# DeepNorm layer with a product-key expert FFN on one core: two index lists, the pace of the row gathers, one engine's order and three late factors

## The chip, the cores and the metric

The kernel runs on one core of one Trainium2 chip. The metric is the device time of one execution in microseconds (us): the median of three timed runs before the change is 1704.05 us (1701.3 to 1706.63). The layer is float32 throughout, 256 tokens of width 2048. A change of less than 0.3%, some 5 us, can't be told from none.

## The reference, cut to what matters

The layer has three parts, each closed by a layer norm: a mixed attention (8 differential and 8 stick-breaking heads), an expert FFN found by product keys, and a gated per-layer embedding. The change lies in the FFN:

```python
def peer_ffn(x, wq, sub_keys, u, v):          # x: 256 tokens of 2048; u, v: 16384 experts of 2048
    q = (xt @ wq).reshape(t, 8, 256)           # 8 heads; halves qa, qb
    va, ia = top_k(qa . sub_keys[0], 16)       # 16 of 128 keys for each half
    vb, ib = top_k(qb . sub_keys[1], 16)
    cand = va[:, None] + vb[None, :]           # 256 pairs
    top, sel = top_k(cand, 16)
    eidx = ia * 128 + ib  at  sel              # 16 experts per token and head
    gates = softmax(top)
    w = gates * gelu(u[eidx] . x)              # 128 experts per token in all
    return sum over those 128 of  w * v[eidx]
```

## The kernel before, in words

**Stages.** The kernel goes once through these stages, and TensorE (PE) has work in each: the attention with its projections and the first norm (0 to 414 us in the profile), the 16 query projections q0 to q15 with the top-k on VectorE (DVE) beside them (414 to 533 us), 68 dense *u blocks* (533 to 864 us), 40 *row blocks* (869 to 1145 us), 86 *v blocks* (1147 to 1590 us, the last three of them in another order, see below), and the closing norm, gate and embedding.

**Two ways to the experts.** Of the 256 tokens the first 88 are *sparse*: for each, the rows u[e] and v[e] of its own experts are fetched from HBM by GpSimd (POOL) with indirect DMAs, the *gathers*, 128 rows of 8 KB (1.05 MB) at a time into one of four `gb` buffers (`NGB`). There are 88 gathers of u rows and then 88 of v rows. DVE consumes each with one instruction over 128x2048 (`use()`): a dot product with x for u (L951), and a weighted sum into `y` for v (L961, the first of a group L959). The other 168 tokens (`NDT`) are *dense*: PE multiplies them with whole blocks of 128 experts. One block is 16 fp32 matmuls of 128x128 by 128x168, which the profile counts as 32.

**u blocks and row blocks.** For the expert blocks 0 to 67 (`SEG1`) u is loaded transposed by SyncE's queue (SP) into the five `wf` buffers, multiplied, and GELU goes to A0 and A1 (`u_block`, L212). Of the other 60 blocks only the experts that some dense token uses are taken: a list of their indices is made on the core, POOL fetches those rows (`uf`, 40 row blocks of 128, `CAPS[1]`), PE transposes them (`ps_T`, L1286), ScalarE (ACT) copies the result to `uT` (L1289), PE multiplies (L1295), and GELU goes to WL.

**Gate factors.** `gate_work` builds for each dense token the matrix of its gate values over (expert block, expert): one-hot rows on DVE (`eq`, `ohb`), scaled on ACT into two fp16 halves `hi` and `lo` (L1048, L1049), a product on PE (`ps_G`), and a DVE multiply into A0 and A1. The result is written to HBM (`s_w0`, 5.9 MB; for the second part `s_w1`, 5.2 MB). This is the *first factor pass* (part 0, beside the row blocks) and the second one (part 1, beside the first v blocks).

**Lists.** `list_work(oh, part)` turns the count of users per expert (`m16`) into a compact list: column sums and ranks on PE and DVE, then 23 groups (part 0) or 20 groups (part 1) of one-hot tiles on DVE (`eqb`, `blk`, `row`) and products on PE (`ps_list`), at last the indices `idxV` (rows of u and v) and `idxW` (rows of `s_w`). Before the change part 1 is made in the u blocks, by the generator `work`, and part 0 in the row blocks, by `listing`.

**v blocks.** For each of 46 + 40 listed blocks (`CAPS`) POOL fetches the factors `wc` (128 rows of 672 B from `s_w`) and the rows `vf` (128 rows of 8 KB from v); a `vf` takes one of the five `wf` buffers, so it is fetched at most four blocks ahead (`LEAD`). For part 1 DVE multiplies wc by WL (`weigh`, L1371), and PE adds 16 products into the six banks `psv` (L1348). The last three blocks (`STAG`) are kept back as `held`: their products are issued bank by bank, so that bank after bank can be closed (`v_out`, L1363), transposed (`res2`, L1421) and taken into the statistics. Ahead of bank 2 stand the *row sums* of the sparse tokens, `third_sums`, which need the finished `y` (L1015).

**What sets the order.** The program is written stage by stage, and generators are advanced inside the block loops: `run(work, n)` does n steps of the side work, and `gathers(p)` adds p to an account and issues one gather (a step of `sparse`) for each whole unit. The paces are the constants `GQ` (q blocks from the fourth), `GU`, `GUF` (u blocks with one step and with more), `GUL`, `GULS` (row blocks up to 27, and later), `GV` (v blocks). Each engine runs its instructions in the order of its own queue. A scheduler chooses that order, except that instructions wrapped in `keep(...)` stay in written order against each other on their engine. Each gather of the u stage is preceded by a tiny `mark` load on SP and a copy on POOL, which tie POOL's place to SP's. SP's queue is in order too: a load that must wait for its buffer holds back all loads behind it. The v stage's loop ends with

```python
        if b == N1 - STAG - 1:            # the last v block ahead of the held ones
            while not run(sparse, 1):     # the rest of the sparse work
                pass
...
    held = [weigh(block)[2:] for block in fetched]
```

Of the kernel before, what the change touches and what calls it, by code (L numbers as in the profile page):

```python
# [13 lines left out]
AF = mybir.ActivationFunctionType  # L14
# [25 lines left out]
SEG1 = 68  # L40
# [4 lines left out]
CAPS = (46, 40)  # L45
# [8 lines left out]
NDT = T - NSP  # L54
# [1 line left out]
NGB = 4  # L56


GQ = 2.1
GU, GUF, GUL, GULS = 0.50, 0.60, 1.40, 1.00  # L60
GV = 0.68
GSCALE = 2.0 ** 15
GB = 3

# [96 lines left out]
def build(tc, a, out):  # L161
# [624 lines left out]
    def topk_work():  # L786
        nc.vector.tensor_copy(io128, io128f)
        for h in range(PH):
            for _ in topk_heads(0, h, 1):
                pass  # L790
            head_slots(h)
            yield
        for i in range(1, len(GROUPS)):
            slots(i, 0, by_slot(i, 0))

        second, first, flags = topk_heads(1, 0, PH), gates(0), first_flags()
        for step in range(24):
            next(second)
            if step > 2:
                next(first, None)  # L800
            next(flags, None)
            yield
        for _ in second:
            next(flags, None)
            yield
        for _ in flags:
            yield
        yield from index_T(1)
        yield from second_flags(gates(1))
# [48 lines left out]
    def second_flags(gating):  # L858

        nonlocal steps  # L860
        pools.close("tk")
        flp = pools.open("flp", "left", bufs=1)
        for dst, src in ((ahead, a["c_svalid"][:, :P]), (ones16, a["c_ones"])):
            src_f = flp.tile([P, P], F32, name="src_f", tag="src_f", bufs=2)
            load(src_f, src)
            nc.gpsimd.tensor_copy(dst, src_f)
        load(lin, a["c_lin"])
        steps = 5
        made = []

        def counts():
            t0, n, ohb, eq = made.pop(0)
            for j in range(n):
                count(t0 + j, ohb[:, j, :], eq[:, j, :])

        for i, t0 in enumerate(range(P, T, GB)):
            n = min(GB, T - t0)
            ohb = flp.tile([P, GB, P], F16, name="ohb", tag="ohb", bufs=OHB)
            eq = flp.tile([P, GB, P], F16, name="eq", tag="eq", bufs=OHB)
            if i % 2:  # L880
                for j in range(n):
                    act_one_hot(eq[:, j, :], flp, niaT[:, t0 + j:t0 + j + 1])
            else:
                keep(nc.vector.tensor_tensor(
                    eq[:, :n], io128[:, None, :].to_broadcast([P, n, P]),
                    iaT[:, t0:t0 + n, None].to_broadcast([P, n, P]), op=ALU.is_equal))
            keep(nc.vector.tensor_tensor(
                ohb[:, :n], io128[:, None, :].to_broadcast([P, n, P]),
                ibT[:, t0:t0 + n, None].to_broadcast([P, n, P]), op=ALU.is_equal))
            made.append((t0, n, ohb, eq))  # L890
            next(gating, None)
            yield
            if len(made) > OHB - 1:
                counts()
        while made:
            counts()
        keep(nc.vector.tensor_scalar(m16, cnt.pop(), 1.0, None, op0=ALU.min))
        for _ in gating:
            pass
        gates_T()  # L900
        steps = 3
        yield
        yield from list_work(flp, 1)

    ys = [None for _ in GROUPS]
    pace = gin.tile([1, 1], F32, name="pace")
# [118 lines left out]
    def gate_work(oh, parts, s0, ns, part, fresh):  # L1025
# [5 lines left out]
        def one_hot(t0, n):  # L1031
            def rows(x, m):
                return x[:, None, :].to_broadcast([P, n, m])

            def cols(x, m):
                return x[:, t0:t0 + n, None].to_broadcast([P, n, m])

            ohb = oh.tile([P, GB, P], F16, name="ohb", tag="ohb", bufs=OHB)
            eq = oh.tile([P, GB, ns], F16, name="eq", tag="eq", bufs=OHB)
            hi = oh.tile([P, GB, ns], F16, name="hi", tag="hi", bufs=OHB)  # L1040
            lo = oh.tile([P, GB, ns], F16, name="lo", tag="lo", bufs=OHB)
            keep(nc.vector.tensor_tensor(eq[:, :n], rows(io128[:, s0:s0 + ns], ns), cols(iaT, ns),  # L1042
                                         op=ALU.is_equal))
            keep(nc.vector.tensor_tensor(ohb[:, :n], rows(io128, P), cols(ibT, P),
                                         op=ALU.is_equal))
            for j in range(n):
                t = slice(t0 + j, t0 + j + 1)
                nc.scalar.mul(hi[:, j, :], eq[:, j, :], ghf[:, t])  # L1048
                nc.scalar.mul(lo[:, j, :], eq[:, j, :], glf[:, t])  # L1049
            return ohb, hi, lo  # L1050

        def product(t0, n, ohb, hi, lo):
# [185 lines left out]
    for ia in range(SEG1):  # L1238
        if ia == EARLY:
            pools.close("earlyp")  # L1240
            a1p = pools.open("a1p", "right", bufs=1)
            A1 = a1p.tile([P, SEG1 - SEG0, NDT], F32, name="A1")
        u_block(ia, W_of(ia))
        run(work, steps)
        gathers(1.5 if ia < EARLY else GU if steps == 1 else GUF)
    while not run(work, 1):
        pass
    pools.close("flp", "tkl")
# [33 lines left out]
    def rows_T(uf, c, pool, tpool):  # L1282

        ps = pbank(pool, "ps_T")
        for j in range(4):
            nc.tensor.transpose(ps[:, j * P:(j + 1) * P],  # L1286
                                uf[:, (4 * c + j) * P:(4 * c + j + 1) * P], ident)
        uT = tpool.tile([P, 512], F32, name="uT", tag="uT", bufs=4 if tpool is utp else 2)
        nc.scalar.copy(uT, ps)  # L1289
        return uT  # L1290

    def rows_mm(ps, uT, c):
# [2 lines left out]
            nc.tensor.matmul(ps[:, :NDT], uT[:, j * P:(j + 1) * P], XF[:, d, NSP:],  # L1295
                             start=d == 0, stop=d == ND - 1)

    def first_part():
        yield from gate_work(ohp, (A0, A1), *PARTS[0], 0, False)

    def first_list():
        yield from list_work(ohp, 0)

    work, listing = first_part(), first_list()
    rows = []
    turned = []

# [12 lines left out]
    for b in range(CAPS[1]):  # L1320
        if b == CAPS[1] - 5:
            while not run(work, 1):
                pass
            while not run(listing, 1):
                pass
            pools.close("a1p", "a0p")
            g2p = pools.open("g2p", "right", bufs=1)
            G2 = g2p.tile([P, SEG2, NDT], F32, name="G2")
            wcp = pools.open("wcp", "right", bufs=1)
        ps = pbank(pp, "ps_u")  # L1330
        for c in range(4):
            turn(4 * b + c + 2)
            rows_mm(ps, turned.pop(0), c)
            if b < CAPS[1] - 5:
                run(work, 1)
        nc.scalar.activation(WL[:, b, :], ps[:, :NDT], AF.Gelu_apprx_tanh)
        if b > 2:
            run(listing, 1)
        if b >= CAPS[1] - 4:
            fetch(wcp)  # L1340
        gathers(GUL if b < 28 else GULS)
# [120 lines left out]
    for b in range(LEAD + 1, N1 - STAG):  # L1462
# [8 lines left out]
        if b == N1 - STAG - 2:  # L1471

            tc.mark_branch_hint_location("rest", "LikelyTaken", [mybir.EngineType.PE])
        if b == N1 - STAG - 1:
            while not run(sparse, 1):
                pass

# [391 lines left out]
```

## Time and profile before

| | |
|---|---|
| median of three runs | 1704.05 us |
| time of the profiled execution, its span | 1705.25 us, 1703.4 us |
| PE busy | 1667.9 us (98%) |
| DVE busy, ACT busy, POOL busy | 1120.4, 754.0, 678.5 us |
| DMA | 533.47 MB, mean 313 GB/s |
| share of the DMA engines' time in POOL's queue | 48.3% |
| granted clock of PE | 0.991 |

The 1.9 us between span and time lie before the first and after the last instruction. PE is busy for 98% of the span, so time can be won or lost almost only where PE stands still or runs at a lower clock, and the profile is to be read by stage: which waits of PE there are, and which queue was late. A busy PE is not always PE at full speed; the column PEclk of the windows tells the granted clock. A DMA share of about 1 means that the 16 DMA engines moved data without a pause.

### The profile page before, as it was taken

What the parts mean: (1) busy time and instruction counts of PE and PEld (TensorE: products, weight loads), DVE (VectorE), ACT (ScalarE), POOL (GpSimd) and SP (SyncE); (2) the same over time, 40 slices, a digit from 0 to 9 for tenths busy, and PEclk for the clock granted to TensorE, in tenths of its full rate; (3) what the DMA queues carried; (4) which work ended last, traced back from release to release, by engine and by line L of the source; (5) the groups of instructions that cost most, each with busy time, mean ns of one, the idle gap of its engine ahead of it and who ended that gap; (6) DMA issues with size and microseconds to landing.
All of it is one profiled execution on the core that took longest, in us unless ns stands there. A gap on an engine that the chain in (4) does not pass through costs nothing.

```text
span 1703.4 us, 29145 instructions
## 1 busy us (share of the span) xinstructions
PE 1667.9 (98%) x11120; PEld 1549.9 (91%) x11120; DVE 1120.4 (66%) x2127; ACT 754.0 (44%) x1883; POOL 678.5 (40%) x605
## 2 busy tenths in 40 slices
PE   9999999999999999999999999999999999997998
PEld 7888888877889999999999999899999999997786
DVE  5565488763499789756768888646774343453776
ACT  5677468753101534366457776435551001000552
POOL 0144023103254423611355434555665778782000
PEclk9999999999999999999999999999999999998999
DMA  8645644484998999897799887999999999996561
GB/s 295 197 153 162 235 160 154 158 317 150 377 393 333 373 420 414 347 383 291 293 396 403 314 340 310 370 423 407 359 379 397 417 415 415 416 406 267 177 262 50
DMA packets 93976, 533.47 MB, mean 313 GB/s; under 512 B 12920, under 2 KB 16168, under 8 KB 41064
## 3 DMA queue, kind: packets, MB, share of 16 engines
q0 software_dynamic: 48912, 327.40, 48.3%
q1 hardware_dynamic: 43192, 201.02, 32.2%
q10 hardware_dynamic: 1728, 3.15, 0.5%
q8 instruction: 89, 1.46, 0.3%
q14 instruction: 55, 0.45, 0.1%
HBM read 515.70 MB, written 15.99 MB: 312 GB/s over the span
## 4 chain that ended last, share of the span: by engine, by line
PE 67%; DMA 13%; DVE 10%; issue 5%; POOL 4%; ACT 1%; POOLq 0%; SPq 0%; ACTq 0%; DVEq 0%
PE ps_v L1348 16%; PE ps_u L1295 9%; PE ps_qk L200 7%; PE ps_u L212 6%; DVE gb L951 4%; PE ps_qk L202 4%; PE ps_T L1286 4%; DMA uf<-u_rows,idxV 3%; PE ps_q L212 3%; DMA gb<-u_rows,eig 3%; DMA vf<-v_rows,idxV 3%; DMA gb<-v_rows,eig 2%; PE ps_v L219 2%; PE ps_v L220 2%; PE ps_v L221 2%
## 5 line engine op out<-in xcount | busy, mean ns | idle before, releaser
L1348 PE MATMUL ps_v<-wc,vf 128*128 128x168 f32 x2752 | 414.3, 310 | 13.5 <-DVE wc L1371 10.5
L1348 PEld LDWEIGHTS ps_v<-wc,vf 128*128 128x128 f32 x2752 | 399.0, 192 | 15.7 <-DVE wc L1371 10.8
L212 PE MATMUL ps_u<-XF,wf 128*128 128x168 f32 x2016 | 303.9, 308 | 1.2 <-DMA wf<-peer_u 1.2
L212 PEld LDWEIGHTS ps_u<-XF,wf 128*128 128x128 f32 x2016 | 288.8, 190 | 2.8 <-DMA wf<-peer_u 1.3
L122 DVE TENSOR_TENSOR wl<-wf,wh 128x1024 fp32r<-128x1024 f32 (+1 forms) x199 | 212.7, 1091 | 104.1 <-ACT wh L121 102.3
L121 ACT CAST wh<-wf 128x1024 fp32r<-128x1024 f32 (+1 forms) x199 | 172.1, 893 | 228.4 <-DMA wf<-ple_gate 114.5
L961 DVE SCALAR_TENSOR_TENSOR y<-gb,ew,y 128x2048 f32<-128x2048 f32 x78 | 182.9, 2345 | 85.9 <-DMA gb<-v_rows,eig 85.6
L951 DVE SCALAR_TENSOR_TENSOR gb<-gb,xq 128x2048 f32<-128x2048 f32 x88 | 203.0, 2318 | 45.9 <-DMA gb<-u_rows,eig 45.7
L1295 PE MATMUL ps_u<-XF,uT 128*128 128x168 f32 x1280 | 213.0, 310 | 0.0
L983 POOL DMA_INDIRECT gb<-u_rows,eig x88 | 113.8, 1294 | 217.2 <-DVE gb L951 111.7
L1295 PEld LDWEIGHTS ps_u<-XF,uT 128*128 128x128 f32 x1280 | 186.3, 191 | 0.4
L200 PE MATMUL ps_qk<-X,wh 128*128 128x512 f32 x512 | 185.2, 401 | 0.0
L983 POOL DMA_INDIRECT gb<-v_rows,eig x88 | 129.6, 1473 | 110.2 <-DVE y L961 44.6
L202 PE MATMUL ps_qk<-X,wl 128*128 128x256 f32 x512 | 145.7, 285 | 0.0
L1048 ACT ACTIVATE hi<-eq,ghf 128x68 f16<-128x68 f16 (+1 forms) x336 | 113.2, 337 | 70.3 <-DVE eq L1042 70.2
L1262 POOL DMA_INDIRECT vf<-v_rows,idxV x86 | 107.0, 1244 | 63.1 <-PE ps_G L1057 30.5
L1289 ACT COPY uT<-ps_T 128x512 f32<-128x512 f32 x160 | 91.3, 580 | 79.5 <-PE ps_T L1286 74.3
L200 PEld LDWEIGHTS ps_qk<-X,wh 128*128 128x128 f32 x512 | 96.4, 188 | 22.0 <-issue 1.0
L1262 POOL DMA_INDIRECT wc<-s_w,idxW x86 | 105.7, 1229 | 26.6 <-issue 24.4
L212 PE MATMUL ps_q<-XF,wf 128*128 128x256 f32 x512 | 113.8, 379 | 0.7 <-ACT eb L581 0.7
L1049 ACT ACTIVATE lo<-eq,glf 128x68 f16<-128x68 f16 (+1 forms) x336 | 112.1, 334 | 0.0
L212 PEld LDWEIGHTS ps_q<-XF,wf 128*128 128x128 f32 x512 | 95.8, 190 | 13.4 <-ACT eb L581 1.1
(335 smaller groups left out, 2601.1 us busy)
## 6 DMA issues: line engine op xcount, KB each, us to landing
wf<-peer_u SPq DMA_DIRECT2D x63, 1024.0 KB
wf<-w_qk SPq DMA_DIRECT2D x64, 512.0 KB
wf<-w_out SPq DMA_DIRECT2D x32, 512.0 KB
wf<-peer_wq SPq DMA_DIRECT2D x16, 1024.0 KB
wf<-ple_gate SPq DMA_DIRECT2D x16, 1024.0 KB
wf<-w_v SPq DMA_DIRECT2D x16, 512.0 KB
wf<-w_sv SPq DMA_DIRECT2D x15, 512.0 KB
early<-peer_u SPq DMA_DIRECT2D x5, 1024.0 KB
```

Of the source, the lines that this page charges most:

```text
L121: self.order(nc.scalar.copy(wh, src))
L122: self.order(nc.vector.tensor_tensor(wl, src, wh.bitcast(F32), op=ALU.subtract))
L200: nc.tensor.matmul(ps, wh[:, j * P:(j + 1) * P], xt[:, dt, :], start=dt == 0, stop=False)
L202: nc.tensor.matmul(ps[:, :T], wl[:, j * P:(j + 1) * P], xt[:, dt, :T], start=False, stop=dt == ND - 1)
L212: nc.tensor.matmul(ps[:, :T - t0], wf[:, dt * P:(dt + 1) * P], xt[:, dt, t0:], start=dt == 0, stop=dt == ND - 1)
L951: keep(nc.vector.scalar_tensor_tensor(g, g, 1.0, xq[i], op0=ALU.mult, op1=ALU.mult, accum_out=eact[i][:, j:j + 1]))
L961: keep(nc.vector.scalar_tensor_tensor(ys[i], g, ew[i][:, j:j + 1], ys[i], op0=ALU.mult, op1=ALU.add))
L983: keep(nc.gpsimd.indirect_dma_start(out=g, out_offset=None, in_=a[kind], in_offset=bass.IndirectOffsetOnAxis(ap=eig[i][:, 0, j:j + 1], axi ...
L1048: nc.scalar.mul(hi[:, j, :], eq[:, j, :], ghf[:, t])
L1262: keep(nc.gpsimd.indirect_dma_start(out=dst, out_offset=None, in_=src, in_offset=bass.IndirectOffsetOnAxis(ap=idx[:, b:b + 1], axis=0)))
L1295: nc.tensor.matmul(ps[:, :NDT], uT[:, j * P:(j + 1) * P], XF[:, d, NSP:], start=d == 0, stop=d == ND - 1)
L1348: return nc.tensor.matmul(psv[d // 3][:, d % 3 * NDT:(d % 3 + 1) * NDT], vf[:, d * P:(d + 1) * P], wc, start=False, stop=last and (d % 3 = ...
```

## The change

It has six edits.

1. *Paces.* The q blocks issue 1.6 instead of 2.1 gathers each, the u blocks 1, then 0.60, then 0.75, and 0.40 in the last eight (before: 1.5, 0.50, 0.60), the row blocks 1.45 up to block 27 and 0.60 after (before: 1.40 and 1.00), the v blocks 0.74 instead of 0.68. The number of gathers is the same, 176.
2. *Top-k work.* While it runs, every second u block does two steps of it instead of one, and there are nine steps, which only hand out flag work, between the end of the top-k of the second 128 tokens and the transposes of its indices.
3. *Lists.* `list_work(flp, 0)` follows `list_work(flp, 1)` in the u blocks at three steps a block; `listing` is gone.
4. *First factor pass.* It is advanced from row block 2 on.
5. *ACT.* `hi`, `lo`, the copy to `uT` and the GELU to WL are kept in written order.
6. *Last v factors.* The blocks that are fetched and not yet multiplied are weighed ahead of the rest of the sparse work.

```diff
-GQ = 2.1
-GU, GUF, GUL, GULS = 0.50, 0.60, 1.40, 1.00
-GV = 0.68
+GQ = 1.6
+GU, GUF, GUT, GUL, GULS = 0.60, 0.75, 0.40, 1.45, 0.60
+GV = 0.74
@@ topk_work
         for _ in second:
             next(flags, None)
             yield
+        for _ in range(9):
+            next(flags, None)
+            yield
@@ second_flags
         yield from list_work(flp, 1)
+        steps = 3
+        yield from list_work(flp, 0)
@@ gate_work, one_hot
-                nc.scalar.mul(hi[:, j, :], eq[:, j, :], ghf[:, t])
-                nc.scalar.mul(lo[:, j, :], eq[:, j, :], glf[:, t])
+                keep(nc.scalar.mul(hi[:, j, :], eq[:, j, :], ghf[:, t]))
+                keep(nc.scalar.mul(lo[:, j, :], eq[:, j, :], glf[:, t]))
@@ u blocks
-        run(work, steps)
-        gathers(1.5 if ia < EARLY else GU if steps == 1 else GUF)
+        run(work, steps + (steps == 1) * (ia % 2))
+        gathers(1 if ia < EARLY else GU if steps == 1 else GUF if ia < SEG1 - 8 else GUT)
@@ rows_T
-        nc.scalar.copy(uT, ps)
+        keep(nc.scalar.copy(uT, ps))
@@ row blocks
-            while not run(listing, 1):
-                pass
...
-            if b < CAPS[1] - 5:
+            if 2 <= b < CAPS[1] - 5:
                 run(work, 1)
-        nc.scalar.activation(WL[:, b, :], ps[:, :NDT], AF.Gelu_apprx_tanh)
-        if b > 2:
-            run(listing, 1)
+        keep(nc.scalar.activation(WL[:, b, :], ps[:, :NDT], AF.Gelu_apprx_tanh))
@@ end of the v blocks
         if b == N1 - STAG - 1:
+            fetched[:] = [weigh(block) for block in fetched]
             while not run(sparse, 1):
                 pass
```

Where instructions stand in the built programs, at three places. First DVE at the end of the v blocks, before the change. L961 is the use of a v gather, L1371 the weighing, L122 the low half of the gate weights, L1363 the closing of a bank; L1480 is a branch, and the row L1491 behind it belongs to a path that isn't taken.

```order
L1371 TENSOR_TENSOR wc<-wc,WL 128x168 x2
L961 SCALAR_TENSOR_TENSOR gb<-gb,ew_4056 128x2048 x2
L1480 COMPARE_AND_BRANCH
L1491 TENSOR_TENSOR wc<-wc,wl 128x168 x20
L1480 UNCONDITIONAL_BRANCH x2
L961 SCALAR_TENSOR_TENSOR gb<-gb,ew_4056 128x2048
L1371 TENSOR_TENSOR wc<-wc,WL 128x168 x2
L122 TENSOR_TENSOR wl<-wf,wh 128x512 x4
L1363 SCALAR_TENSOR_TENSOR XF<-XF,ps_v 128x3x168 x2
```

The same place after it (the lines are numbered anew: L966, L1366, L1358).

```order
L1366 TENSOR_TENSOR wc<-wc,WL 128x168 x2
L966 SCALAR_TENSOR_TENSOR gb<-gb,ew_4056 128x2048 x2
L1476 COMPARE_AND_BRANCH
L1487 TENSOR_TENSOR wc<-wc,wl 128x168 x20
L1476 UNCONDITIONAL_BRANCH x2
L966 SCALAR_TENSOR_TENSOR gb<-gb,ew_4056 128x2048
L122 TENSOR_TENSOR wl<-wf,wh 128x512 x4
L1358 SCALAR_TENSOR_TENSOR XF<-XF,ps_v 128x3x168 x2
```

The two weighings that stood behind the last use of a gather are now ahead of the last three uses; the closing of the banks stands behind the last use as before.

Second, POOL at the same place, before the change: L1262 fetches factors and rows of a v block, L983 is a gather.

```order
L983 DMA gb<-v_rows,eig_4054 128x2048
L1262 DMA wc<-s_w_61,idxW_7698 128x168
L1262 DMA vf<-v_rows,idxV_7697 128x2048
L983 DMA gb<-v_rows,eig_4054 128x2048
L1480 COMPARE_AND_BRANCH
```

And after it (L1267, L988).

```order
L988 DMA gb<-v_rows,eig_4054 128x2048
L1267 DMA wc<-s_w_61,idxW_7397 128x168
L1267 DMA vf<-v_rows,idxV_7396 128x2048
L988 DMA gb<-v_rows,eig_4054 128x2048 x2
L1476 COMPARE_AND_BRANCH
```

Behind the last fetch of a v block there are now two gathers instead of one.

Third, SP's queue in the u blocks, before the change. The loads at L281 bring constants for the lists (`src_f`, `lin`); the first takes the place of a table that the top-k on DVE reads to its end. The u load ahead of them is that of block 36.

```order
L111 DMA wf<-peer_u 128x2048 x2
L980 DMA mark<-c_iota 1x1
L111 DMA wf<-peer_u 128x2048
L281 DMA src_f<-c_svalid 128x128
L281 DMA src_f<-c_ones 128x128
L281 DMA lin<-c_lin 128x68
L111 DMA wf<-peer_u 128x2048
```

After it, the u load ahead of `src_f` is that of block 26.

```order
L111 DMA wf<-peer_u 128x2048
L985 DMA mark<-c_iota 1x1
L281 DMA src_f<-c_svalid 128x128
L111 DMA wf<-peer_u 128x2048
L281 DMA src_f<-c_ones 128x128
L281 DMA lin<-c_lin 128x68
L111 DMA wf<-peer_u 128x2048
```

The constants have moved ten u blocks ahead, and with them the place at which SP's loads stand behind the end of the top-k.

More of the change, by code (lines that the diff above doesn't have):

```diff
@@ L1296, in rows_mm @@
                              start=d == 0, stop=d == ND - 1)
[L1298 to L1304, printed above, removed]
+    work = gate_work(ohp, (A0, A1), *PARTS[0], 0, False)
     rows = []
```

## The prediction

> **What bounds the kernel now.** I read the page's first lines, then PE's waits, the windows, and the timelines at the places where PE waits.
>
> ```profile
> span 1703.4 us, 29145 instructions
> PE 1667.9 (98%) x11120; PEld 1549.9 (91%) x11120; DVE 1120.4 (66%) x2127; ACT 754.0 (44%) x1883; POOL 678.5 (40%) x605
> ...
> PE ps_v L1348 <- DVE wc L1371: 10.5, 1, 10.5
> PE ps_T L1286 <- DMA uf<-u_rows,idxV: 6.5, 4, 3.2
> PE ps_v L1348 <- DMA vf<-v_rows,idxV: 2.7, 3, 1.2
> ...
> PE ps_u L212 <- DMA wf<-peer_u: 1.2, 1, 1.2
> ```
>
> The waits' columns are total us, times, longest. PE is busy for 98% and its work stays the same, so only waits can be won: 10.5 us ahead of the held blocks, 6.5 for fetched u rows, 2.7 for fetched v rows, 1.2 for a u load. The windows (us; busy time of PE, PEld, DVE, ACT, POOL; granted clock; DMA share; GB/s) show where the DMA is the partner:
>
> ```profile
> 1093.00:1104.00 11.00, 7.79 (x52) 7.56 (x51) 2.35 (x1) 3.24 (x6) 4.70 (x5) 0.89 1.02 424
> 1104.00:1120.00 16.00, 15.26 (x111) 14.94 (x111) 4.70 (x2) 5.52 (x11) 2.82 (x3) 0.97 1.02 427
> ...
> 1180.00:1290.00 110.00, 110.00 (x958) 108.17 (x957) 77.89 (x144) 63.08 (x258) 71.27 (x59) 1.00 0.97 371
> ...
> 1400.00:1500.00 100.00, 100.00 (x703) 99.42 (x702) 47.36 (x50) 4.43 (x8) 79.58 (x59) 1.00 1.02 415
> 1500.00:1520.00 20.00, 20.00 (x142) 20.00 (x141) 8.67 (x12) 0.00 (x0) 16.34 (x13) 1.00 1.00 398
> 1520.00:1540.00 20.00, 20.00 (x143) 20.00 (x142) 8.45 (x8) 0.00 (x0) 15.47 (x13) 1.00 1.01 411
> ```
>
> Late in the v blocks PE and DMA are both full: 703 matmuls in 100 us are 142 ns each, 4.55 us for a block of 32, at 415 GB/s. Earlier (1180 to 1290) factor products lengthen the blocks, and the DMA moves only 371.
>
> **Start of the row blocks.**
>
> ```profile
> POOL gb L983 <- DVE eqb L1166: 20.4, 4, 12.3
> ...
> 858.13 1.19 POOL L1277 DMA_INDIRECT uf<-u_rows,idxV  x1 [0.30 <-issue]
> ...
> PE ps_T L1286 <- DMA uf<-u_rows,idxV: 2.2, 1, 2.2
> ```
>
> POOL's gathers lag behind the list on DVE, the first `uf` goes out at 858.1, and PE waits 2.2 us for it (the last row is the window 855 to 875). After the change both lists end some seven blocks ahead of the row blocks, and the last u blocks pace 0.40 gathers, so POOL is free when the buffer is, about two u blocks earlier: -2.2. If it is still late, 0. Part 0's list costs PE the same in either stage; I cost its move at nothing, because PE shows no wait for the list that is made there already. Without DVE's room there, PE's list products would hold back u blocks.
>
> **End of the row blocks.**
>
> ```profile
> 1079.77 8.89 SPq L281 DMA_DIRECT2D s_w<-A  x9
> ...
> PE ps_T L1286 <- DMA uf<-u_rows,idxV: 4.3, 3, 3.2
> ...
> L1175 DVE TENSOR_TENSOR row<-io,rank 128x384 f16<-128x384 f16 (+1 forms) x23 | 12.7, 554 | 16.7 <-PE ps_G L1057 16.7
> ```
>
> SP's factor write starts at 1079.8; then the DMA is full (424, 427), PE waits 4.3 us for `uf` (window 1080 to 1130), and at clocks 0.89 and 0.97 it loses 7.79 x 0.11 + 15.26 x 0.03 = 1.3 us more: 5.6. Before, each block brings a `uf` and a gather, 2.1 MB, beside the 5.9 MB written, plus gathers that DVE's list work made late (its `row` tiles alone take 12.7 us). After, a block brings 1.05 x 1.60 = 1.7 MB and nothing is late. Five blocks of 6.3 us at 415 GB/s move 13 MB; they need 16.4 before and 14.3 after, and `uf` runs four blocks ahead. I take -5.6, between that and 0. The later first pass moves the write by two blocks, still ahead of its first reader. ACT in written order: copies to `uT` already stand between `hi` and `lo`, and PE has no wait for ACT there, so nothing.
>
> **Middle of the u blocks.** SP stands until DVE is through the top-k:
>
> ```profile
> SPq L281 <- DVE ibN L731: 15.3, 1, 15.3
> ...
> 635.86 4.89 SPq L111 DMA_DIRECT2D wf<-peer_u  x2
> ...
> 697.75 0.33 SPq L281 DMA_DIRECT2D src_f<-c_svalid  x1
> ...
> 699.13 0.38 SPq L111 DMA_DIRECT2D wf<-peer_u  x1
> ...
> 706.67 5.54 PE L212 MATMUL ps_u<-XF,wf 128*128 128x168 f32 x37 [1.16 <-DMA wf<-peer_u]
> ...
> 539.60:697.30 157.70, 157.70 (x1124) 157.16 (x1124) 135.07 (x331) 64.25 (x189) 63.68 (x81) 1.00 0.94 377
> ...
> 539.60:697.30 157.70, 68.55 (x58) 1.00 0.94 377
> ```
>
> The last row is L951 alone on DVE (two records a gather, 29 gathers). Of 157.7 us DVE is busy for 135.1, 66.5 of them with other work than gathers, and idle for 22.6. After the change 17 uses stand in the same stretch of its queue: 66.5 + 17 x 2.36 = 106.7, plus 3 to 22.6 idle. I take 8, since 12 gathers fewer compete: the top-k ends at 654. SP meets `src_f` behind the load of block 26 (635.86), stands until 654, and block 27's load goes out at 655 and lands 7.5 us later (699.13 to 706.67), at 663. PE wants block 27 five blocks of 4.6 us after 635.9, at 659, and 1.5 later for flag counts that now come earlier. It waits 2.3 instead of 1.2: +1.1; between -1.2 and +15.
>
> **The v blocks.** Paces summed up: before, 13 x 2.1 + 5 x 1.5 + 37 x 0.50 + 26 x 0.60 + 28 x 1.40 + 12 x 1.00 = 120 gathers stand ahead of the v blocks; after, 13 x 1.6 + 5 + 25 x 0.60 + 30 x 0.75 + 8 x 0.40 + 28 x 1.45 + 12 x 0.60 = 114 (the top-k's steps now end at u block 29). Six more, 62, fall to the v blocks. POOL's gathers by window:
>
> ```profile
> 1147.30:1304.40 157.10, 24.66 (x22) 1.00 0.98 382
> 1304.40:1560.00 255.60, 59.22 (x35) 0.98 1.00 408
> ```
>
> At 1304 31 blocks are done. After the change 31 x 0.74 = 23 gathers are done there, 39 are left instead of 35. A block needs 1.049 + 0.086 MB for `vf` and `wc`, and per 4.55 us that is 406 GB/s with 0.68 gathers, 420 with 0.74. The first is under the 415 that the DMA brings, and the backlog of the second factor write drains until about 1500 (398 and 411 behind that); the second isn't, so the last gather lands later by 4 x 1.049 MB / 414 = 10.1 us, less 1.0 for the slack in those two windows: +9.1. The other end is 0, if the DMA has more to give.
>
> **Last v factors.**
>
> ```profile
> 1557.40 2.35 DVE L961 SCALAR_TENSOR_TENSOR gb<-gb,ew 128x2048 f32<-128x2048 f32 x1 [7.44 <-DMA gb<-v_rows,eig]
> 1559.67 0.57 DVE L1371 TENSOR_TENSOR wc<-wc,WL 128x168 f32<-128x168 f32 x2
> 1560.15 2.49 DVE L122 TENSOR_TENSOR wl<-wf,wh 128x512 fp32r<-128x512 f32 x4
> 1564.93 0.68 DVE L1363 SCALAR_TENSOR_TENSOR XF<-XF,ps_v 128x504 f32<-128x504 f32 x1 [2.29 <-PE ps_v L1348]
> ...
> 1560.05 7.93 PE L1348 MATMUL ps_v<-wc,vf 128*128 128x168 f32 x34 [10.52 <-DVE wc L1371]
> 1567.82 0.38 PE L1421 MATMUL ps_y<-ident,XF 128*128 128x128 f32 x2
> ```
>
> The last gather lands at 1557.4; DVE uses it, weighs, PE does 34 matmuls of banks 0 and 1, and the transposes start at 1567.82, 10.4 us after the landing. With the weighing ahead, PE does these matmuls before the landing. But the transposes need a closed bank, and that stands behind the last use: 2.35 + 2.49 + 0.68 = 5.5 us after the landing, -4.9. So the wait isn't removed, it moves behind the 34 matmuls. They took 7.93 us instead of 34 x 0.142 = 4.8; that loss of clock, 3.1 us, now falls on the row sums, in whole or not: 0 to +3.1, +1.5 taken, since their 32 columns keep PE less busy. By the Trainium skill ("TensorE: Matmul & The Clock Gate", Part 1) the clock halves after an idle window of about 3.4 us and is back after as long a busy one, which would cost 1.7 us, and the sum would be 0.2 higher; the measured 3.1 is the larger, and I keep to the rows.
>
> **Sum** against the profiled execution's 1705.25: -2.2 - 5.6 + 1.1 + 9.1 - 4.9 + 1.5 = -1.0, so 1704.2. That execution was 1.2 above the median, so 1703 us.
>
> **Rivals.**
> *The DMA carries the faster pace.* The windows at 424 and 427 GB/s are above the 420 needed. Against it: those hold SP's direct writes, and POOL's gathers alone got 415. Then the +9.1 goes: 1694. The Trainium skill ("DMA: Bandwidth & Descriptors", Specifications) gives a ceiling of 435 GB/s, by which this rival would hold; no window here reached it.
> *SP stands too long* (slower). If DVE idles in the top-k as before, 22.6 us, that ends at 669, block 27 lands at 678 and PE waits 17 us: up to 1718. It decides from about 14 us idle, where the top-k ends at 661 and the time passes 1709. Against it: 17 of those 22.6 us were waits for gathers, and there are fewer.
> *The row blocks' waits stay*, because write and `uf` still meet: +5.6, 1709.
>
> **Numbers.** Forecast 0.45, by itself 1697 to 1709; DMA carries it 0.28; SP 0.12; rows 0.10; 0.05 for others, such as ACT's written order holding up PE. What a measurement can tell from no change is 0.3%, about 5 us. Faster: 0.27 from the DMA rival, 0.10 from the forecast's low end and the rest, 0.37. Slower: 0.10 from SP, 0.05 from the rows, 0.06 from the high end and the rest, 0.21. Same: 0.42. The range 1690 to 1712 reaches into the first two rivals.
>
> **What would show it.** PE without the 2.2 us at the first row block and the 4.3 us near 1100; a wait of 0 to 6 us for `wf` about 660; DMA at 414 or more from the second factor write to the last landing, and that landing some 9 us later, counted from v block 31; PE waiting ahead of L1416 (after) rather than for `wc`, for 11 us or so. A last gather that lands with v block 82, or a wait for `wf` over 9 us, would prove me wrong.

## Result, and the profile after

The changed kernel took 1713.0 us (median of five executions, 1708.9 to 1713.9) against 1703.8 for the kernel before (1701.3 to 1706.6): 1.0051 times as long, with a 95% interval of 1.0034 to 1.0068. It is slower, where no change was forecast, and 1 us above the range of 1690 to 1712. Eleven more executions in another session had a median of 1711.0 and a ratio of 1.0032 (1.0018 to 1.0047). The profiled execution was the fastest of the first five, 1708.9 us, so a second profile was taken of each kernel, and numbers below are given for both.

The page's span, and the waits of PE (total us, times, longest):

```profile
span 1706.6 us, 29204 instructions
...
PE ps_v L1343 <- DMA vf<-v_rows,idxV: 14.4, 6, 9.5
PE ps_y L1416 <- DVE XF L1358: 4.3, 2, 3.2
PE ps_T L1291 <- DMA uf<-u_rows,idxV: 3.0, 1, 3.0
PE ps_v L1343 <- DVE wc L1366: 1.8, 2, 1.1
```

The wait of 10.5 us for the weighed factors is gone, as is that for a u load. The 4.3 us for `uf` at the end of the row blocks are gone too. The waits for fetched v rows have grown from 2.7 to 14.4 us, and one of 3.0 for the first `uf` stands where 2.2 stood.

Where the time went is seen by cutting both executions at the same places of the program. The windows of the kernel before run from u block 0 to row block 0, to v block 0, from v block 31 to DVE's last use of a gather, and from there to the end (us; busy time of PE, PEld, DVE, ACT, POOL; granted clock; DMA share; GB/s):

```profile
533.30:868.90 335.60, 332.24 (x2456) 327.25 (x2455) 257.91 (x577) 155.54 (x465) 116.17 (x136) 1.00 0.90 355
868.90:1147.30 278.40, 274.07 (x2302) 268.83 (x2301) 205.45 (x399) 174.03 (x514) 136.44 (x94) 0.99 0.91 365
...
1304.40:1557.40 253.00, 242.12 (x1692) 240.38 (x1690) 100.53 (x91) 6.61 (x12) 182.82 (x139) 0.99 1.01 412
1557.40:1703.40 146.00, 134.17 (x674) 112.72 (x674) 96.92 (x175) 56.91 (x113) 6.38 (x10) 0.92 0.44 155
```

The same stretches of the changed kernel:

```profile
532.60:872.70 340.10, 337.07 (x2503) 330.75 (x2502) 283.40 (x679) 147.83 (x437) 111.15 (x132) 1.00 0.90 348
872.70:1140.20 267.50, 267.50 (x2252) 264.38 (x2251) 171.12 (x302) 182.63 (x549) 132.11 (x98) 1.00 0.97 387
1140.20:1297.50 157.30, 157.30 (x1335) 153.82 (x1334) 107.59 (x183) 80.02 (x328) 104.79 (x82) 1.00 0.93 358
1297.50:1562.80 265.30, 248.83 (x1712) 245.71 (x1711) 110.74 (x97) 6.60 (x12) 192.44 (x143) 0.98 1.01 411
1562.80:1706.60 143.80, 131.92 (x656) 110.29 (x654) 96.28 (x173) 56.88 (x113) 6.36 (x10) 0.93 0.45 158
```

Up to v block 0 the change wins 6.4 us: +4.5 in the u blocks, -10.9 in the row blocks. They are lost again behind v block 31, +12.3, and the end gives 2.2 back. In that stretch the DMA works at 412 GB/s in the one kernel and at 411 in the other; by these rates it moves 104.2 MB before and 109.0 MB after. In the first 31 v blocks of the changed kernel, in between, the rate is only 358 GB/s. The gathers that POOL issued ahead of and behind v block 31:

```profile
1140.20:1297.50 157.30, 27.46 (x22) 1.00 0.93 358
1297.50:1566.00 268.50, 64.96 (x39) 0.98 0.99 406
```

Behind v block 31 it is 39 instead of 35. The table gives the same cuts for every profile that was taken; its columns are us, the gathers left at v block 31, and the ratio to the kernel before in the same session with its interval. "Last use" is DVE's last use of a gather, "end" the end of the span. e7 and e10 are one execution each, so they have no ratio.

| kernel | u 0 to row 0 | row 0 to v 0 | v 0 to v 31 | v 31 to last use | last use to end | left | ratio |
|---|---|---|---|---|---|---|---|
| before | 335.7 | 278.3 | 157.1 | 253.0 | 146.0 | 35 | 1 |
| e7, before again | 334.6 | 277.8 | 157.1 | 256.3 | 145.2 | 35 | |
| after | 340.2 | 267.5 | 157.3 | 265.2 | 143.9 | 39 | 1.0051 (1.0034 to 1.0068) |
| e1, after again | 340.6 | 267.5 | 157.3 | 265.6 | 143.9 | 39 | 1.0032 (1.0018 to 1.0047) |
| e2, v pace 0.68 | 340.1 | 267.5 | 157.3 | 275.3 | 144.6 | 41 | 1.0110 (1.0091 to 1.0129) |
| e3, v pace 0.90 / 0.65 | 341.3 | 268.5 | 156.8 | 261.0 | 143.9 | 35 | 1.0010 (0.9998 to 1.0022) |
| e4, before + edit 6 | 337.9 | 277.6 | 157.1 | 256.1 | 141.1 | 35 | 0.9997 (0.9985 to 1.0009) |
| e5, v pace 1.20 / 0.90 / 0.56 | 339.6 | 269.5 | 163.8 | 242.2 | 148.3 | 29 | 0.9979 (0.9962 to 0.9996) |
| e6, list 0 in the rows | 334.4 | 281.8 | 157.3 | 266.0 | 142.3 | 39 | 1.0065 (1.0047 to 1.0082) |
| e8, ACT not ordered | 341.8 | 276.3 | 157.3 | 267.2 | 142.3 | 39 | 1.0062 (1.0044 to 1.0081) |
| e9, v paces around the write | 343.0 | 268.7 | 162.8 | 240.8 | 146.5 | 33 | 0.9910 (0.9886 to 0.9933) |
| e10, no last u gathers | 337.0 | 267.8 | 157.3 | 278.1 | 144.3 | 42 | |
| e11, without edit 6 | 340.9 | 268.8 | 157.3 | 266.0 | 144.7 | 40 | 1.0038 (1.0019 to 1.0057) |
| e12, before + paces of e9 | 338.4 | 277.4 | 155.5 | 227.5 | 162.7 | 30 | 0.9935 (0.9916 to 0.9953) |

The two profiles of the kernel before agree within 1.1 us in the u and row blocks and within 3.3 behind v block 31, those of the changed kernel within 0.4. But e4 and e12, which differ from the kernel before only in the v blocks, took 337.9 and 338.4 us in the u blocks where it took 335.7 and 334.6: there a difference of less than 4 us between two kernels says nothing. What lies ahead of u block 0, which no edit but the q pace touches, differs by up to 4.6 us between executions.

### The profile page after: what moved, and what is told of

Its sections match the earlier page's. It is cut to its first block, busy times and chain, and to the rows that moved or that the text cites. A ratio compares the mean times of both kernels' runs of the same rounds, so it can differ in the third digit from the quotient of the medians.

```text
span 1706.6 us, 29204 instructions
## 1 busy us (share of the span) xinstructions
PE 1670.6 (98%) x11120; PEld 1552.5 (91%) x11120; DVE 1120.8 (66%) x2127; ACT 752.7 (44%) x1883; POOL 688.6 (40%) x603
## 5 line engine op out<-in xcount | busy, mean ns | idle before, releaser
L1343 PE MATMUL ps_v<-wc,vf 128*128 128x168 f32 x2752 | 416.0, 311 | 16.5 <-DMA vf<-v_rows,idxV 14.4
L212 PE MATMUL ps_u<-XF,wf 128*128 128x168 f32 x2016 | 309.5, 310 | 0.0
L122 DVE TENSOR_TENSOR wl<-wf,wh 128x1024 fp32r<-128x1024 f32 (+1 forms) x199 | 212.8, 1093 | 104.2 <-ACT wh L121 103.1
L966 DVE SCALAR_TENSOR_TENSOR y<-gb,ew,y 128x2048 f32<-128x2048 f32 x78 | 182.9, 2344 | 96.6 <-DMA gb<-v_rows,eig 96.0
L988 POOL DMA_INDIRECT gb<-u_rows,eig x88 | 112.5, 1279 | 214.2 <-DVE gb L956 136.0
L202 PE MATMUL ps_qk<-X,wl 128*128 128x256 f32 x512 | 146.0, 285 | 0.0
L988 POOL DMA_INDIRECT gb<-v_rows,eig x88 | 124.0, 1409 | 36.4 <-issue 16.5
L1267 POOL DMA_INDIRECT vf<-v_rows,idxV x86 | 105.8, 1230 | 64.3 <-PE ps_G L1062 31.5
L1267 POOL DMA_INDIRECT wc<-s_w,idxW x86 | 112.3, 1306 | 34.1 <-issue 25.3
```

What stands on the lines that cost most here:

```text
L122: self.order(nc.vector.tensor_tensor(wl, src, wh.bitcast(F32), op=ALU.subtract))
L202: nc.tensor.matmul(ps[:, :T], wl[:, j * P:(j + 1) * P], xt[:, dt, :T], start=False, stop=dt == ND - 1)
L212: nc.tensor.matmul(ps[:, :T - t0], wf[:, dt * P:(dt + 1) * P], xt[:, dt, t0:], start=dt == 0, stop=dt == ND - 1)
L966: keep(nc.vector.scalar_tensor_tensor(ys[i], g, ew[i][:, j:j + 1], ys[i], op0=ALU.mult, op1=ALU.add))
L988: keep(nc.gpsimd.indirect_dma_start(out=g, out_offset=None, in_=a[kind], in_offset=bass.IndirectOffsetOnAxis(ap=eig[i][:, 0, j:j + 1], axi ...
L1267: keep(nc.gpsimd.indirect_dma_start(out=dst, out_offset=None, in_=src, in_offset=bass.IndirectOffsetOnAxis(ap=idx[:, b:b + 1], axis=0)))
```

## Experiments

**The changed kernel again (e1).** No edit.

> The changed kernel again, for a second profile. Its profiled execution took 1708.9 us, the four others 1712.6 to 1713.9. Theory A (the DMA is the bound from v block 31 to the last landing): 1711 to 1714 us, and the second profile has the same row blocks (no wait for uf but the first) and a last landing 12 us or more later, counted from v block 31, than the kernel before. Theory B (something that varies outside the v blocks, such as SP's stand for the top-k): the extra 4 to 5 us show as a wait for wf or uf ahead of row block 0.

1711.0 us, and the second profile (1713.8 us) has the stretches of the first within 0.4 us. It is 5 us longer, 4.0 of it because u block 0 starts at 536.6 instead of 532.6. So theory A holds for the change, and B is out: no wait for `wf` or for a second `uf` appears, and this execution is slower ahead of u block 0, before any work of the u or v blocks.

**The old v pace (e2).**

```diff
-GV = 0.74
+GV = 0.68
```

> The changed kernel with the v pace back at 0.68. Theory A (what counts is how many gathers are left at v block 31, since the DMA is full from there): 41 instead of 39 are left, 2.1 MB or 5 us more at 414 GB/s: 1716 to 1720 us. Theory C (the pace of 0.74 is itself the fault, it crowds the fetches of v rows, for which PE waited 14.4 us in six places): those waits go and the time falls to 1700 to 1707 us.

1722.7 us, above the 1716 to 1720 of theory A and far from C's 1700 to 1707. By the paces the slower one leaves six gathers for the time behind the last paced block; PE waits less for `vf`, but it waits at the end for the closing of a bank, which stands behind the last gather's use:

```profile
PE ps_y L1416 <- DVE XF L1358: 21.4, 2, 20.3
PE ps_v L1343 <- DMA vf<-v_rows,idxV: 10.1, 5, 6.0
```

Two gathers more cost 10 us from v block 31 to the last use, where 5 were worked out from bytes alone: POOL issued the leftover in a bunch behind the last `vf`, in part only as buffers came free, and the rate over the stretch fell from 411 to 402 GB/s. So C is out: the pace of 0.74 was not in itself the fault.

**Early v gathers (e3).**

```diff
-GV = 0.74
+GVE, GV = 0.90, 0.65
...
         v_blocks(1, wcp, half)
-        gathers(GV)
+        gathers(GVE if b < 31 else GV)
```

> The changed kernel with v paces of 0.90 in the first 31 v blocks and 0.65 after: 34 instead of 39 gathers are left at v block 31. Theory A: the DMA has room there (358 GB/s in the first 31 blocks, against 415 later), the last landing comes 5 x 1.049 MB / 414 = 12.7 us earlier, counted from v block 31, the waits for vf go, and the time is 1698 to 1703 us. Theory C: 0.90 crowds the fetches already in the first 31 blocks, with the second factor write (5.9 MB) on top, and waits of 10 us or more for vf appear there: 1713 us or more.

1705.5 us: 5.5 won over the changed kernel, where A said 8 to 13, and no crowding ahead of v block 31 (C). 35 gathers were left, as in the kernel before, and the stretch still took 261 us. The factor write, at about v block 29 (5.2 MB; the expectation took the size of the first one), meets more traffic than in the changed kernel, 404 against 384 GB/s in the 100 us ahead of v block 31, and PE loses 6.0 us to `vf` directly behind it:

```profile
PE ps_v L1343 <- DMA vf<-v_rows,idxV: 6.0, 5, 4.0
```

(window 1290 to 1345). In the 40 us ahead of 1540 the DMA moved 378 GB/s; the pace of 0.65 asks for 399, worked out as in the prediction, and the DMA share reads 0.99 there, so whether the pace or the DMA was the limit isn't shown. Bytes left over a rate of 414 give the last landing only if that rate is held to the end.

**Edit 6 alone, on the kernel before (e4).**

```diff
         if b == N1 - STAG - 1:
+            fetched[:] = [weigh(block) for block in fetched]
             while not run(sparse, 1):
```

> The kernel before with the last v factors weighed ahead of the rest of the sparse work, and nothing else. The step as predicted: the 34 matmuls of the held blocks run ahead of the last landing, the transposes start 5.5 instead of 10.4 us behind it, and 1.5 of that comes back as a slower clock: -3.4 us, 1700.4. Rival 1: the path behind the landing is the same and nothing is won, 1703 to 1705. Rival 2: the clock loss is the larger of the two, 1705 to 1707.

1704.4 against 1705.1 us: no difference (Rival 1). The path behind the last landing did become shorter as forecast, 141.1 us instead of 145.2 and 146.0. But PE, which no longer waits for the weighing, now waits for the held blocks' rows themselves:

```profile
1558.05 7.57 PE L1348 MATMUL ps_v<-wc,vf 128*128 128x168 f32 x32 [6.07 <-DMA vf<-v_rows,idxV]
1566.80 0.44 PE L1421 MATMUL ps_y<-ident,XF 128*128 128x128 f32 x2 [1.18 <-DVE XF L1363]
```

They land only 3.3 us ahead of the last gather, since the DMA brings both late. Counted from v block 31 the last use comes after 256.1 us, between the 253.0 and 256.3 of the two profiles of before, so the edit doesn't delay it; what this profile lost, 2.2 to 3.3 us, lies in the u blocks, ahead of the edit. By the stretches the edit is worth some 3 us, by the times of twelve executions nothing (0.9985 to 1.0009); this difference stays open.

**Earlier still (e5).**

```diff
-GU, GUF, GUT, GUL, GULS = 0.60, 0.75, 0.40, 1.45, 0.60
-GV = 0.74
+GU, GUF, GUT, GUL, GULS = 0.60, 0.75, 0.40, 1.55, 0.60
+GV1, GV2, GV = 1.20, 0.90, 0.56
...
-        gathers(GV)
+        gathers(GV1 if b < 12 else GV2 if b < 31 else GV)
```

> The changed kernel with row-block pace 1.55 instead of 1.45 and v paces of 1.20 in the first 12 v blocks, 0.90 up to block 30 and 0.56 after: by program 28 instead of 39 gathers are left at v block 31. Theory A (bytes left at v block 31 over a rate of 415 GB/s): 106.0 MB were moved behind it with 35 left (0.90/0.65), so 28 leave 98.7 MB, 238 us, which is as long as PE needs for the 52 blocks (237 us); the waits for vf behind v block 31 and the wait ahead of L1416 go down to a few us, 1692 to 1698 us. Theory D (the last landing is set by the last fetches and gathers themselves, which are issued about v block 81 and need some 16 us each time): the landing comes no earlier than 10 us behind v block 83, 1700 to 1706 us. Theory C (early crowding): a wait of 5 us or more for vf or uf ahead of v block 31.

1703.0 us (1695.0 to 1709.5), 0.9979 of the kernel before; the profiled execution took 1697.3. 29 gathers were left. The last use is now 8 us ahead of v block 83, so D is out: nothing ties the last landing to the last fetches. But the early pace has its price: the first 31 blocks took 163.8 us instead of 157.3, with blocks of 6.4 and 8.5 us at v blocks 18 and 19, and one of 9.0 followed at v block 34. It isn't C's crowding by C's own sign: ahead of v block 31 PE has no wait for `vf` or `uf`, only 4.0 us that the profile puts down to no engine, and what held those blocks isn't shown. A's 1692 to 1698 came out in three of twelve executions.

**List 0 back in the row blocks (e6).**

```diff
-        steps = 3
-        yield from list_work(flp, 0)
...
-    work = gate_work(ohp, (A0, A1), *PARTS[0], 0, False)
+    work, listing = gate_work(ohp, (A0, A1), *PARTS[0], 0, False), list_work(ohp, 0)
...
+            while not run(listing, 1):
+                pass
...
+        if b > 2:
+            run(listing, 1)
```

> The changed kernel with the list of part 0 back in the row blocks. By the prediction the move costs PE nothing in sum: the stretch from u block 0 to row block 0 becomes about 5 us shorter than the 340 us of the changed kernel, that from row block 0 to v block 0 about 5 us longer than 267.5, and the time stays within 3 us of 1711. The wait of 3 us for the first uf goes, if it came from gathers that wait for the list's work on DVE: then 1708. Rival (the list in the row blocks delays the gathers, and so the write and uf meet again): 4 to 6 us of waits for uf about row block 33, 273 + 5 = 278 us for the row blocks as in the kernel before, 1713 to 1717.

1717.8 us. The u blocks became 6 us shorter, as forecast, the row blocks 14.3 longer instead of 5. Neither cause given was right: `uf` and the factor write do not meet, and the wait for the first `uf` stays at 2.2 us. ACT's waits in the row blocks (868.6 to 1150.4) point to another:

```profile
ACT hi L1051 <- DVE eq L1045: 46.4, 22, 3.9
```

In written order a copy to `uT` must not pass a `hi` that waits for DVE's `eq`; with the list's work on DVE, `eq` is late 22 times, and PE is held up behind the copies. In the changed kernel that row reads 2.2 us in three times. In the kernel before, where a copy could pass, it was 8.9. Some of the 14.3 us is also the list's own work on PE, which came back into the row blocks.

**The kernel before again (e7).** No edit.

> The kernel before again, for a second profile: the last landing 251 to 255 us behind v block 31, the row blocks 277 to 280 us, from u block 0 to row block 0 334 to 338 us. If the stretches of one kernel differ by more than 3 us between two profiles, a difference of that size between kernels says nothing.

1706.0 us, one execution. All stretches are as expected, the last landing at the upper end of its range (table).

**ACT's order taken away (e8).**

```diff
-                keep(nc.scalar.mul(hi[:, j, :], eq[:, j, :], ghf[:, t]))
-                keep(nc.scalar.mul(lo[:, j, :], eq[:, j, :], glf[:, t]))
+                nc.scalar.mul(hi[:, j, :], eq[:, j, :], ghf[:, t])
+                nc.scalar.mul(lo[:, j, :], eq[:, j, :], glf[:, t])
...
-            keep(nc.scalar.copy(uT, ps))
+            nc.scalar.copy(uT, ps)
...
-        keep(nc.scalar.activation(WL[:, b, :], ps[:, :NDT], AF.Gelu_apprx_tanh))
+        nc.scalar.activation(WL[:, b, :], ps[:, :NDT], AF.Gelu_apprx_tanh)
```

> The changed kernel without ACT's written order (edit 5). By the prediction that order is worth nothing: 1709 to 1713 us, row blocks 266 to 269 us. Rival (the order is what made the row blocks shorter): row blocks of 272 us or more, with PE waiting for ACT's uT.

1718.3 us, and 276.3 us for the row blocks: the rival holds. With both lists done, the one-hots are ready before the row blocks start, and the scheduler puts `hi` and `lo` ahead of the copies that PE waits for. ACT at row block 0, where nine of them stand ahead of the first copy:

```profile
871.47 0.35 ACT L1053 ACTIVATE hi<-eq,ghf 128x68 f16<-128x68 f16 x1 [2.87 <-DVE eq L1047]
...
873.42 0.34 ACT L1053 ACTIVATE hi<-eq,ghf 128x68 f16<-128x68 f16 x1
873.66 0.56 ACT L1294 COPY uT<-ps_T 128x512 f32<-128x512 f32 x1
```

Row block 0 takes 9.4 us instead of 6.4, and the last two, where the second pass comes in, 8.5 and 9.1 instead of 6.3 and 7.5. These three make 6.8 of the 8.8 us. PE's waits show only 3.4 us in the row blocks; PE counts as busy for 5.6 us more than in the changed kernel (267.50):

```profile
874.30:1150.60 276.30, 273.08 (x2242) 267.77 (x2243) 168.54 (x300) 182.08 (x555) 140.57 (x96) 0.99 0.95 370
```

**The v paces around the factor write (e9).**

```diff
-GU, GUF, GUT, GUL, GULS = 0.60, 0.75, 0.40, 1.45, 0.60
-GV = 0.74
+GU, GUF, GUT, GUL, GULS = 0.60, 0.75, 0.40, 1.55, 0.60
+GV1, GV2, GV3, GV = 1.00, 0.85, 0.30, 0.72
...
-        gathers(GV)
+        gathers(GV1 if b < 12 else GV2 if b < 28 else GV3 if b < 38 else GV)
```

> The changed kernel with row-block pace 1.55 and v paces that leave the DMA to the second factor write: 1.00 in v blocks 0 to 11, 0.85 to 27, 0.30 in 28 to 37, 0.72 after; by program 33 gathers are left at v block 31. In every kernel so far PE waited for vf about v blocks 33 to 37, behind that write. Theory A with the write (the DMA's time is shared out, first come first served): those waits of 3 to 9 us shrink to under 2 us, the last landing comes about (69.3 + 33 x 1.049) MB / 415 = 250 us behind v block 31, 5 us behind v block 83, and the time is 1692 to 1699 us. Rival (the sum of bytes decides, wherever they stand): the waits move to another place, v block 31 to the last landing stays at 255 or more, 1701 to 1706 us.

1692.3 us (1686.1 to 1697.0), 0.991 of the kernel before, the fastest of all. Behind v block 31 the windows and PE's waits (1308 to the end) read:

```profile
1307.80:1548.60 240.80, 240.80 (x1690) 240.04 (x1688) 90.58 (x86) 4.43 (x8) 167.94 (x136) 1.00 1.01 405
...
PE ps_v L1343 <- DVE wc L1366: 2.6, 1, 2.6
PE ps_v L1343 <- DMA vf<-v_rows,idxV: 1.7, 1, 1.7
```

PE has no wait between v block 31 and the last use, which comes 240.8 us behind it instead of 265. That is earlier than the 250 worked out, since the stretch moved 97.5 MB (405 GB/s) and not 103.9. In which order the DMA serves its queues, which the expectation assumes, no run shows. The early 1.00 and 0.85 cost 5.5 us ahead of v block 31 (two blocks of 9.1 and 7.2 us, in one of which PE waited 2.7 for DVE).

**No gathers in the last u blocks (e10).**

```diff
-GU, GUF, GUT, GUL, GULS = 0.60, 0.75, 0.40, 1.45, 0.60
+GU, GUF, GUT, GUL, GULS = 0.60, 0.75, 0.00, 1.45, 0.60
```

> The changed kernel with no gathers in the last eight u blocks (GUT 0.00 instead of 0.40). If the first uf is late because gathers stand ahead of it on POOL: its wait of 3.0 to 3.5 us goes to under 1, and from u block 0 to row block 0 it is 336 to 338 us instead of 340.3. If POOL's lag comes from the lists' work on DVE, which ended at 837 us with gathers waiting behind it, it stays at 2 us or more. Either way 3 gathers more are left at v block 31, and the last landing is 271 to 275 us behind it instead of 265: 1716 to 1722 us.

1719.4 us, one execution. The wait for the first `uf` is gone and the u blocks take 337.0. POOL in the changed kernel, and then in this one:

```profile
861.19 3.05 POOL L988 DMA_INDIRECT gb<-u_rows,eig  x1 [0.24 <-DVE gb L956]
864.55 2.13 POOL L1282 DMA_INDIRECT uf<-u_rows,idxV  x1 [0.30 <-issue]
```

```profile
849.76 0.96 POOL L988 DMA_INDIRECT gb<-u_rows,eig  x1 [0.16 <-issue]
851.07 1.92 POOL L1282 DMA_INDIRECT uf<-u_rows,idxV  x1 [0.35 <-PE ps_u L212]
```

So the fetches stood behind gathers on POOL, and those behind DVE. Three gathers more were left at v block 31, and the last use came 12.7 us later, more than the 6 to 10 expected: again a bunch behind the last block.

**The changed kernel without edit 6 (e11).** The inverse of e4's edit.

> The changed kernel without the weighing ahead (edit 6). As predicted it is worth 3.4 us: from the last use of a gather to the end 147 instead of 143.9 us, and 1713 to 1716 us against the changed kernel's 1711. As the kernel before with that edit alone had it (0.9997 of the time of before): no difference, 1709 to 1713 us.

1712.2 us and 1.0038, as with it (1.0032). The end of its v blocks:

```profile
1569.58 7.02 PE L1343 MATMUL ps_v<-wc,vf 128*128 128x168 f32 x34 [17.83 <-DVE wc L1366]
1576.44 0.38 PE L1416 MATMUL ps_y<-ident,XF 128*128 128x128 f32 x2
```

The transposes start 9.5 us behind the last use; with the edit it is 5.4. From the last use to the end only 0.8 of these 4.1 us remain: the row sums take 10.2 us here, 12.7 and 13.1 in the two profiles of the changed kernel.

**The kernel before with e9's v paces (e12).**

```diff
-GV = 0.68
+GV1, GV2, GV3, GV = 1.00, 0.85, 0.30, 0.72
...
-        gathers(GV)
+        gathers(GV1 if b < 12 else GV2 if b < 28 else GV3 if b < 38 else GV)
```

> The kernel before with the v paces of the run around the factor write (1.00, 0.85, 0.30, 0.72), and nothing else of the change. It separates what the v paces are worth from what the edits ahead of the v blocks are worth. If the two add up: the changed kernel's u and row blocks took 607.7 us together (340.2 + 267.5) against 614.0 and 612.4 in the two profiles of before, so this kernel is about 5 us slower than the 1692.3 of the changed kernel with those paces: 1696 to 1700 us. Rival (the row blocks of before leave gathers and a factor write behind, which the higher early v pace meets): PE waits 5 us or more for vf ahead of v block 31, and the gain over the kernel before is under 3 us, 1703 to 1706.

1695.4 us, 0.9935: the v paces alone bring most of what e9 brings, and the rival, with 1703 to 1706, is out. The intervals of e9 and e12 meet, so the times don't show that the rest of the change is worth anything there. By the profiles e9 is 8.7 us shorter in the row blocks and 4.6 longer in the u blocks. And the early pace was too high for this kernel: it left only 30 gathers, the last use is 24 us ahead of v block 83, and v blocks 31 to 34 lose 10 us behind the factor write. PE's waits:

```profile
PE ps_T L1286 <- DMA uf<-u_rows,idxV: 6.6, 3, 2.6
PE ps_v L1348 <- DMA vf<-v_rows,idxV: 6.3, 2, 3.3
```

## Why the prediction was wrong

It forecast -1.0 us on the profiled execution. The stretches of the two profiles of each kernel, averaged, give -5.3 us from u block 0 to v block 0 (predicted -6.7), +0.2 for the first 31 v blocks, +10.8 from there to the last use (+9.1) and -1.7 behind it (-3.4): +4.0. That the first five executions showed +9.2 and the next eleven +5.9 is partly the scatter ahead of u block 0 that e1 shows; the forecast's own error is these 5 us, and no single term made them. Three steps made the time longer than forecast: POOL was not free at the first row block (-2.2 taken, +0.8 in the first pair of profiles), the excess of the v blocks was larger (+9.1 taken, +10.8 measured), and so was the loss of clock in the row sums (+1.5 taken, +3.3 and +3.0). A fourth, that ACT's order is worth nothing, failed without showing in the sum. That the stretch up to v block 0 came out only 1.4 us off is luck in part: the u blocks up to row block 0 were forecast at -1.1 and gave +5.3, the row blocks at -5.6 and gave -10.6. By its steps:

- *Start of the row blocks, -2.2:* wrong, +0.8 (3.0 against 2.2 us of wait; in the second profiles 3.5 against 1.2). "POOL is free when the buffer is" was the step that failed. DVE ended the lists at 837 us, in u block 61, some seven blocks ahead as forecast. But by then the uses of gathers, and so the gathers on POOL, had fallen behind, and the last of them held POOL up to 864. e10 shows it: without the gathers of the last eight u blocks the wait is gone.
- *End of the row blocks, -5.6:* right. The changed kernel has no wait and a clock of 1.00 there. Of the two reasons given, fewer gathers and a list that is no longer late, the first is enough: e6 has the list back in the row blocks and no wait for `uf` there either.
- *List move, first pass and ACT order at nothing:* about right in sum, wrong in the parts. From u block 0 to v block 0 PE is busy for 606.3 us before (332.24 + 274.07) and for 604.6 after (337.07 + 267.50): most of the 6.6 us that went from the row blocks stands in the u blocks, where the list's products now are. "PE has no wait for ACT there, so nothing" was the step that failed. It was read from a kernel in which the one-hots come late; once the lists are done early, the order is worth 8.8 us in the row blocks (e8). With the order and without the move they are 14.3 us longer (e6), of which the u blocks give 6 back. So the two edits need each other: the move makes the one-hots ready early, the order keeps them from passing the copies. With both, nearly every row block takes 6.8 us with factor products and 6.3 without, in place of 6.3 to 7.8. The first pass alone wasn't tried, nor the order alone on the kernel before.
- *Middle of the u blocks, +1.1:* the steps were right, one size was not. Up to the end of the top-k DVE was busy for 107.8 us (106.7 worked out) and idle for 4.2 instead of 8. So the top-k ended at 651 rather than 654, the load of block 27 went out at 651.3, and PE, which began that block at 659.8, had no wait: -1.2, at the end of the range given:

```profile
650.90 0.33 SPq L281 DMA_DIRECT2D src_f<-c_svalid  x1
```

- *The v blocks, +9.1:* right in kind, somewhat short: +12.3 in the first pair of profiles, +9.3 in the second. The rate was 411 GB/s, as in the kernel before (412, and 407 in e7; 414 used), and the excess 4.8 MB instead of 4.2. Whether there was the 1.0 of slack that was subtracted isn't shown, since the two pairs differ by 3.0. The rival in which the DMA carries the faster pace is out: the most that any 100 us of the v blocks showed in any kernel is 418 GB/s (420 in the u blocks of the kernel before). The Trainium skill's ceiling of 435 GB/s ("DMA: Bandwidth & Descriptors", Specifications), by which that rival would have held, was reached in no window of 10 us or more.
- *Last v factors, -4.9 and +1.5:* the path was right, the loss of clock mis-sized. The changed kernel, DVE's last use and PE's transposes:

```profile
1557.91 7.08 PE L1343 MATMUL ps_v<-wc,vf 128*128 128x168 f32 x32 [9.48 <-DMA vf<-v_rows,idxV]
...
1562.76 2.35 DVE L966 SCALAR_TENSOR_TENSOR gb<-gb,ew 128x2048 f32<-128x2048 f32 x1 [0.21 <-DVEq L1476]
...
1568.17 0.43 PE L1416 MATMUL ps_y<-ident,XF 128*128 128x128 f32 x2 [3.17 <-DVE XF L1358]
```

5.4 us, as worked out. But the row sums behind it took 12.7 us instead of 9.3. The windows of the row sums before, and then those of the changed kernel: PE's wait for the bank, the row sums, and the matmuls behind them:

```profile
1568.03:1572.60 4.57, 4.57 (x44) 4.57 (x42) 1.01 (x2) 0.37 (x1) 0.00 (x0) 1.00 0.13 54
1572.60:1577.34 4.74, 4.74 (x24) 4.74 (x24) 0.00 (x0) 0.00 (x0) 0.00 (x0) 0.51 0.00 0
```

```profile
1565.00:1568.17 3.17, 0.00 (x1) 0.00 (x1) 3.17 (x7) 0.00 (x0) 1.68 (x3) 1.00 0.37 83
1568.44:1569.50 1.06, 1.06 (x12) 1.06 (x11) 0.64 (x2) 0.37 (x1) 0.00 (x0) 0.95 1.18 278
1569.50:1581.09 11.59, 11.59 (x56) 11.59 (x56) 0.00 (x0) 0.00 (x0) 0.00 (x0) 0.50 0.34 104
1581.09:1586.30 5.21, 5.21 (x20) 5.16 (x21) 0.55 (x1) 0.00 (x0) 0.00 (x0) 0.50 0.00 0
```

In both kernels the full clock comes during the matmuls of the held blocks and lasts 6.8 us (1565.8 to 1572.6 before, 1562.6 to 1569.4 after). Before, most of that falls on the row sums. With the edit PE spends 3.2 us of it waiting for the bank, and it ends 0.9 us into them. The loss is 3.3 us, not 1.5 (3.0 in the second profiles). It isn't the edit's alone: in e4, where the bank is waited for only 1.2 us, the row sums take 10.4 us, against 9.3 and 10.1. In the times neither e4 nor e11 finds the edit worth anything that can be measured.

The paces are where the change loses: fewer gathers ahead of the v blocks leave four more behind v block 31. e9, with more of them in the row blocks and in the first 28 v blocks, and few about the factor write, is 1.2 to 1.4% faster than the changed kernel by the ratios (0.991 against 1.0032 and 1.0051). What the gap about the write is worth by itself wasn't tried; e5, without one and with fewer gathers left, was slower (0.9979).

## What to carry to other kernels

When PE and DMA are both full in a late stage, count the bytes still to come at its start, and move them into earlier stretches where the rate is below what the DMA has shown; watch what the early stretch pays for it, and where a large write falls in between. Compare the lengths of equal blocks, not only the waits: a copy that comes a little late showed as longer busy time (e8). Where one stage became shorter, look whether its work only moved to another. An edit that makes work ready earlier lets a scheduler put it ahead of something urgent, so such a move and an ordering can each be harmful alone and good together (e6, e8).

## What the runs showed of the hardware

PE's granted clock fell to half in the middle of the row sums of the kernel before (1.00 up to 1572.6, 0.51 after) although by the records PE had no idle time there, and in the changed kernel it stayed at 0.50 through 11.6 us of row sums and 5.2 us of matmuls of 168 columns before it came back. By the Trainium skill ("TensorE: Matmul & The Clock Gate", Part 1) some 3.4 us of sustained work bring the full clock back; 11.6 us of these matmuls of 32 columns, between which the records leave PE no idle time, did not, so the trace differs from the rule there. Why they did not isn't shown.
